# Expert biases of a mixture-of-experts kernel: split in column quarters on 128 partitions and put in place by transfers

## The chip, the cores and the metric

The kernel runs on one core of a Trainium2 chip. The core has five engines with a queue of instructions each: TensorE (PE, matmuls; PEld is its weight load), VectorE (DVE), ScalarE (ACT), GpSimd (POOL) and SyncE (SP), and 16 DMA engines that move what the queues of SP and POOL ask for. Each queue is worked off in the order in which the program was written; engines wait for each other by semaphores. The metric is the time of one execution in microseconds on the device. Line numbers (L130) are those of the kernel before.

## The reference, cut to what matters

One layer for 512 tokens of width 1024: an RMS norm, a projection to four head groups (stick-breaking attention, RG-LRU, HGRN2, Mamba-2), the projection `w_out`, a residual, and then a mixture of 32 experts, four for each token, and a last norm. The biases of the experts come in here:

```python
def run_block(args):
    tok, e = args
    hmid = xt[tok] @ w_gu[e] + b_gu[e]        # b_gu: (32, 2048)
    glu = jnp.minimum(hmid[:, 0::2], SWIGLU_LIMIT)
    lin = jnp.clip(hmid[:, 1::2], -SWIGLU_LIMIT, SWIGLU_LIMIT)
    act = glu * jax.nn.sigmoid(SWIGLU_ALPHA * glu) * (lin + 1.0)
    return act @ w_down[e] + b_down[e]        # b_down: (32, 1024)
```

## The kernel before

The work has a mixer part (about the first 330 us) and an expert part (the rest). The expert part streams the weights of all 32 experts through a ring of buffers (`wch`, 1 MB each) on the SP queue, and multiplies them on PE.

A bias is added by a matmul: a column of ones and zeros that picks the expert, times a table of the biases with the experts on the partitions. For the accuracy of float32 the table of `b_gu` is kept in three bf16 parts that add up to the value: `bgu` is 96 x 2048, part s of expert e on partition 32 s + e. `b_down` is kept in two rounded parts, `bd`, 96 x 1024: the upper part on partitions 0 to 31 and again on 32 to 63, the remainder on 64 to 95. `bgu` is read first by L174, at 318.6 us, `bd` first by L470, at 368.9 us.

`moe_biases` (L119 to L151) makes both tables in the mixer part. Its staging buffer `st` is the ring tile `hg`, 128 x 2048 float32. It loads the 32 rows of a bias three times, one under the other, so that each part is made where it has to lie: for each half of 1024 columns of `b_gu`, ACT rounds 96 rows (L138), DVE subtracts (L139), ACT rounds rows 32 to 63 and 64 to 95 (L141, L142), DVE subtracts on rows 64 to 95 (L143), ACT rounds these (L145). `b_down` is loaded over the first half and made by one ACT and one DVE instruction (L149, L150). The loads go through the POOL queue.

The function is a generator: at each `yield` the program goes on with another. In which order it does is written out by hand, a letter for a step. `m` is `moe_biases`:

```python
ORD1 = 'lcxpvcluelldblllelpmddbcepddssmssmddmbsmddmssm'
ORD2 = 'wnwnwnwwonowwowowwo'
...
emit(ORD1, {"x": xc_silu(), **cgen, "n": nA, "e": c_end(), "l": sL, "d": d_loop(), "s": c_state(), "b": sB,
            "m": moe_biases(tc, a, bp, hg, r_)})
```

Seven `m` stand in `ORD1`. Between them: `d`, the Mamba-2 loop (DVE multiplies the decays by scores, L1874; PE multiplies, L1880; after four rounds DVE makes `y`, L1885 and L1886); `s`, the HGRN2 state (PE L1899, L1906, L1912, L1919; ACT copies `kn`, L1901; DVE updates the state, L1925); `b`, the RG-LRU's norm (ACT L1465, L1466, L1471; DVE L1468, L1472). A letter whose generator is used up does nothing. What is left of the generators after `ORD1` is run out, `b` last but one, ahead of `m`. Then `ORD2` mixes the multiplication by `w_out` (`w`: ACT L1817 and DVE L1818 split 128 x 512 of the weights in two, PE L1823 multiplies) with two norms.

After `ORD2`, SP loads `x` into `acc` (L1958), what the router needs (L98, L100, L102), and then the first expert weights (L159); POOL makes the router's constants (from L69). The router writes the staging buffer `hg` again (L283, first at 290.8 us).

Of the kernel before, what the change touches and what calls it, by code (L numbers as in the profile page):

```python
# [21 lines left out]
F32 = mybir.dt.float32  # L22
FR = mybir.dt.float32r
BF = mybir.dt.bfloat16
I32 = mybir.dt.int32
U32 = mybir.dt.uint32
AF = mybir.ActivationFunctionType
OP = mybir.AluOpType
# [89 lines left out]

def moe_biases(tc, a, bp, st, r_):  # L119

    nc = tc.nc
    bgu = bp.tile([96, 2048], BF, name="bgu")
    bd = bp.tile([96, D], FR, tag="yS", name="bd")
    r_["b"] = bgu, bd
    bst = [st[0:96, 0:1024], st[0:96, 1024:2048]]

    def load(f):
        src = a["moe_b_down"][0] if f == 2 else a["moe_b_gu"][0, :, 1024 * f:1024 * f + 1024]
        for s in range(3):
            nc.gpsimd.dma_start(bst[f % 2][32 * s:32 * s + 32, :], src)  # L130

    load(0)
    load(1)
    yield
    for f in range(2):
        cols = slice(1024 * f, 1024 * f + 1024)
        b = bst[f]
        nc.scalar.activation(bgu[:, cols], b, AF.Copy)  # L138
        nc.vector.tensor_tensor(b, b, bgu[:, cols], op=OP.subtract)  # L139
        yield  # L140
        nc.scalar.activation(bgu[32:64, cols], b[32:64, :], AF.Copy)  # L141
        nc.scalar.activation(bgu[64:96, cols], b[64:96, :], AF.Copy)  # L142
        nc.vector.tensor_tensor(b[64:96, :], b[64:96, :], bgu[64:96, cols], op=OP.subtract)  # L143
        yield
        nc.scalar.activation(bgu[64:96, cols], b[64:96, :], AF.Copy)  # L145
        if f == 0:
            load(2)
    yield
    nc.scalar.activation(bd, bst[0], AF.Copy)  # L149
    nc.vector.tensor_tensor(bd[64:96, :], bst[0][64:96, :], bd[64:96, :].bitcast(F32), op=OP.subtract)  # L150
    yield  # L151


# [898 lines left out]
def tile_kernel(ctx, tc, a, out):  # L1052
# [837 lines left out]
    def c_state():  # L1890
# [3 lines left out]
        for c in range(NT):  # L1894
# [19 lines left out]
            if c < NT - 1:  # L1914
# [13 lines left out]

    emit(ORD1, {"x": xc_silu(), **cgen, "n": nA, "e": c_end(), "l": sL, "d": d_loop(), "s": c_state(), "b": sB,
                "m": moe_biases(tc, a, bp, hg, r_)})  # L1930
    bgu, bd = r_["b"]
    oC = r_["oC"]
# [94 lines left out]
```

## Time and profile before

| | |
|---|---|
| median of 3 runs | 1378.11 us (1372.44 to 1380.81) |
| the profiled execution | 1376.71 us |
| its span, first to last instruction | 1374.9 us |
| mean granted TensorE clock | 0.977 |
| PE / DVE / ACT / POOL busy | 1312.0 / 882.4 / 643.6 / 94.4 us |

Outside the span lie 1.8 us of the profiled execution. Busy times are sums over stages that differ; the views below are cut to the stage that holds the change. In the timeline, several neighbours of one kind can be merged into one row (x4), and rows can overlap by the end of a pipeline. A granted clock of 1.00 is 2.4 GHz, 0.50 is 1.2 GHz.

### The profile page before, as it was taken

The page shows a single profiled execution, that of the slowest core. Times are in us where ns is not written, and L with a number is a line of the kernel's source. Part 1 is how long each engine was busy: PE and PEld are TensorE (multiplying, and loading weights), DVE is VectorE, ACT ScalarE, POOL GpSimd, SP SyncE. Part 2 cuts the span into 40 slices and gives each one's busy share as a digit, 9 for nine tenths or more (in the row PEclk, how much of TensorE's full clock was granted, in tenths as well). Part 3 has the DMA queues.
Part 4 walks back from the last instruction along what each step waited for, and adds up shares of the span by engine and source line. Part 5 has one row for each costly group of instructions (what it writes and reads, how often), then busy time and mean ns, then how long its engine had stood idle before and what let it go on. Part 6 is the DMA issues. An engine that isn't in the chain of part 4 may idle for free.

```text
span 1374.9 us, 17788 instructions
## 1 busy us (share of the span) xinstructions
PE 1312.0 (95%) x6460; PEld 768.3 (56%) x6460; DVE 882.4 (64%) x1215; ACT 643.6 (47%) x886; POOL 94.4 (7%) x162
## 2 busy tenths in 40 slices
PE   7999998898999999999999999999999999999994
PEld 6877773574365554456545655546544555464651
DVE  5457867675576754457546765748545667686865
ACT  5366667652154533336234542526334445454632
POOL 0000123020110002000010000200010000000001
PEclk9999997899999999999999999999999999999998
DMA  6312012087899999888999999999999999999982
GB/s 196 116 61 92 1 70 88 1 325 306 338 398 405 420 419 397 339 363 310 404 366 419 419 394 420 409 419 405 419 400 419 419 393 420 418 417 399 419 359 78
DMA packets 80801, 442.09 MB, mean 322 GB/s; under 512 B 10972, under 2 KB 25380, under 8 KB 31684
## 3 DMA queue, kind: packets, MB, share of 16 engines
q1 hardware_dynamic: 76708, 427.66, 77.7%
q0 software_dynamic: 3856, 12.72, 2.7%
q8 instruction: 52, 0.85, 0.3%
q10 hardware_dynamic: 144, 0.52, 0.1%
q14 instruction: 41, 0.34, 0.1%
HBM read 436.68 MB, written 4.19 MB: 321 GB/s over the span
## 4 chain that ended last, share of the span: by engine, by line
PE 77%; DMA 7%; DVE 7%; ACT 5%; issue 3%; POOL 1%; DVEq 0%; SPq 0%; ACTq 0%; POOLq 0%
PE h L629 18%; PE hL L658 14%; PE m L629 10%; PE m L729 7%; PE m L1198 6%; PE h L789 6%; DMA wch<-in_moe_w_down_dram 4%; DMA wch<-in_moe_w_gu_dram 3%; PE h L658 2%; DVE w L614 1%; PE h L1823 1%; PE m L1823 1%; PE h L696 1%; PE m L1202 1%; PE h L585 1%
## 5 line engine op out<-in xcount | busy, mean ns | idle before, releaser
L614 DVE TENSOR_TENSOR w<-wch,w 128x1024 fp32r<-128x1024 f32 x312 | 378.8, 1224 | 153.8 <-ACT w L613 145.5
L613 ACT ACTIVATE w<-wch 128x1024 fp32r<-128x1024 f32 x312 | 328.4, 1061 | 273.4 <-DMA wch<-in_moe_w_down_dram 98.7
L629 PE MATMUL h<-w,xx 128*72 128x512 f32 (+6 forms) x1248 | 301.9, 399 | 4.9 <-DVE w L614 4.5
L629 PEld LDWEIGHTS h<-w,xx 128*72 128x72 f32 (+6 forms) x1248 | 195.6, 159 | 102.8 <-DVE w L614 7.2
L658 PE MATMUL hL<-wch,xp 128*64 128x512 f32 (+1 forms) x1152 | 239.1, 593 | 1.1 <-DMA wch<-in_moe_w_gu_dram 1.1
L658 PEld LDWEIGHTS hL<-wch,xp 128*64 128x64 f32 (+1 forms) x1152 | 74.8, 134 | 148.8 <-issue 141.2
L729 PE MATMUL m<-wch,aTL 128*64 128x512 f32 x544 | 124.3, 603 | 0.2 <-DVE tg L557 0.2
L629 PE MATMUL m<-w,aH 128*72 128x512 f32 (+6 forms) x416 | 116.5, 400 | 3.4 <-ACT w L613 2.1
L675 ACT ACTIVATE ag<-ag 128x512 f32<-128x512 f32 (+7 forms) x46 | 28.6, 622 | 167.9 <-DVE ag L674 167.8
L629 PEld LDWEIGHTS m<-w,aH 128*72 128x72 f32 (+6 forms) x416 | 62.9, 158 | 39.7 <-issue 7.4
L565 POOL CAST ix<-tg 64x1 int32<-64x1 f32 (+8 forms) x31 | 19.0, 611 | 848.3 <-DVE tg L557 839.7
L791 DVE TENSOR_TENSOR acc<-acc,h 128x1024 f32<-128x1024 f32 (+1 forms) x61 | 72.9, 1198 | 6.4 <-PE h L789 6.4
L729 PEld LDWEIGHTS m<-wch,aTL 128*64 128x64 f32 x544 | 37.0, 138 | 69.2 <-issue 67.2
L763 DVE SCALAR_TENSOR_TENSOR yS<-m,tg,yS 64x512 fp32r<-64x512 f32 (+1 forms) x38 | 28.5, 750 | 71.4 <-ACT yS L761 71.0
L1198 PE MATMUL m<-uH,wh 128*128 128x512 f32 x176 | 71.9, 408 | 0.8 <-DVE uL L1305 0.8
L1198 PE MATMUL m<-uH,wl 128*128 128x512 f32 x176 | 70.1, 398 | 0.5 <-DVE wl L1164 0.4
L1198 PE MATMUL m<-uL,wh 128*128 128x512 f32 x176 | 69.9, 397 | 0.0
L629 PE MATMUL m<-w,aL 128*72 128x512 f32 (+6 forms) x208 | 65.1, 394 | 0.0
L761 ACT ACTIVATE yS<-m,tg 64x512 fp32r<-64x512 f32 (+1 forms) x38 | 25.9, 681 | 74.9 <-PE m L729 72.4
L789 PE MATMUL h<-yS,S 128*128 128x512 f32 (+1 forms) x168 | 54.9, 400 | 2.4 <-DVE acc L791 1.3
L674 DVE TENSOR_SCALAR ag<-hL 128x512 f32<-128x512 f32 (+1 forms) x18 | 11.9, 659 | 64.5 <-PE hL L658 64.5
L1164 DVE TENSOR_TENSOR wl<-wnat,wh 128x1024 fp32r<-128x1024 f32 (+1 forms) x26 | 31.5, 1223 | 30.3 <-ACT wh L1163 30.3
(500 smaller groups left out, 1634.0 us busy)
## 6 DMA issues: line engine op xcount, KB each, us to landing
wch<-in_moe_w_gu_dram SPq DMA_DIRECT2D x256, 1024.0 KB
wch<-in_moe_w_down_dram SPq DMA_DIRECT2D x127, 1024.0 KB
wnat<-in_w_in_dram SPq DMA_DIRECT2D x12, 1024.0 KB
wch<-in_w_out_dram SPq DMA_DIRECT2D x4, 1024.0 KB
xin<-in_x_dram SPq DMA_DIRECT2D x4, 512.0 KB
acc<-in_x_dram SPq DMA_DIRECT2D x4, 512.0 KB
xdr<-wch POOLq DMA_DIRECT2D x4, 512.0 KB, 7.5
out_dram<-fo SPq DMA_DIRECT2D x3, 512.0 KB
```

The costliest lines, as they stand in the source:

```text
L613: nc.scalar.activation(wh, w, AF.Copy)
L614: nc.vector.tensor_tensor(wl, w, wh.bitcast(F32), op=OP.subtract)
L629: nc.tensor.matmul(ps_[q], x, w[:, 512 * q:512 * q + 512], start=start and z == 0, stop=stop and z == 2)
L658: nc.tensor.matmul(u.h[q], u.xT[:, k, :], W[:, 512 * q:512 * q + 512], start=False, stop=last)
L675: nc.scalar.activation(g, g, AF.Gelu_apprx_sigmoid)
L729: nc.tensor.matmul(u.y[0][64 * dh:64 * dh + 64, :], u.aT[:, 2 * (f // 4) + f % 2, (f // 2) % 2, :], W[:, 512 * dh:512 * dh + 512], start=f ...
L763: nc.vector.scalar_tensor_tensor(u.yS[o_, dh, :], y[s_, :], u.gate[s_, :], u.yS[s_, dh, :].bitcast(F32), op0=OP.mult, op1=OP.subtract)
L789: nc.tensor.matmul(hh[:, 512 * dh:512 * dh + 512], s, y, start=z == 0, stop=z == len(todo) - 1)
L791: nc.vector.tensor_tensor(o, o, hh[:, cols], op=OP.add)
L1164: nc.vector.tensor_tensor(wl, w, wh.bitcast(F32), op=OP.subtract)
L1198: nc.tensor.matmul(s.p, s.ws[q // 2][:, k, :], u_[:, k, :], start=(k == 0 and q == 0), stop=(k == KD - 1 and q == 2))
L1823: nc.tensor.matmul(p, m_(x, k)[:, 128 * i:128 * i + 128], ww, start=(k == 0 and q == 0), stop=(k == KD - 1 and q == 2))
```

## The change

The bias rows are loaded once: columns 512 q to 512 q + 511 of `b_gu` go to partitions 32 q to 32 q + 31 of `g`, columns 256 q to 256 q + 255 of `b_down` to the same partitions of `d`. All 128 partitions then hold a quarter each, and the parts of all 2048 columns are made by three ACT and two DVE instructions of 512 columns (`b_down`: one each, 256 columns) in spare columns of the staging buffer. 24 transfers from SBUF to SBUF, 12 on SP's queue for `bgu` and 12 on POOL's for `bd`, put each quarter of each part on its partitions. The generator has four steps in place of seven, so the last three `m` of `ORD1` do nothing.

```diff
-    bst = [st[0:96, 0:1024], st[0:96, 1024:2048]]
-
-    def load(f):
-        src = a["moe_b_down"][0] if f == 2 else a["moe_b_gu"][0, :, 1024 * f:1024 * f + 1024]
-        for s in range(3):
-            nc.gpsimd.dma_start(bst[f % 2][32 * s:32 * s + 32, :], src)
-
-    load(0)
-    load(1)
+    g, d = st[:, 0:512], st[:, 512:768]
+    parts = st[:, 768:1536].bitcast(BF).rearrange("p (s f) -> p s f", s=3)
+    dH, dL = st[:, 1536:1792].bitcast(FR), st[:, 1792:2048].bitcast(FR)
+    for q in range(4):
+        nc.gpsimd.dma_start(g[32 * q:32 * q + 32, :], a["moe_b_gu"][0, :, 512 * q:512 * q + 512])
+        nc.gpsimd.dma_start(d[32 * q:32 * q + 32, :], a["moe_b_down"][0, :, 256 * q:256 * q + 256])
     yield
-    for f in range(2):
-        cols = slice(1024 * f, 1024 * f + 1024)
-        b = bst[f]
-        nc.scalar.activation(bgu[:, cols], b, AF.Copy)
-        nc.vector.tensor_tensor(b, b, bgu[:, cols], op=OP.subtract)
-        yield
-        nc.scalar.activation(bgu[32:64, cols], b[32:64, :], AF.Copy)
-        nc.scalar.activation(bgu[64:96, cols], b[64:96, :], AF.Copy)
-        nc.vector.tensor_tensor(b[64:96, :], b[64:96, :], bgu[64:96, cols], op=OP.subtract)
-        yield
-        nc.scalar.activation(bgu[64:96, cols], b[64:96, :], AF.Copy)
-        if f == 0:
-            load(2)
+    nc.scalar.activation(parts[:, 0, :], g, AF.Copy)
+    nc.scalar.activation(dH, d, AF.Copy)
+    nc.vector.tensor_tensor(g, g, parts[:, 0, :], op=OP.subtract)
+    nc.vector.tensor_tensor(dL, d, dH.bitcast(F32), op=OP.subtract)
     yield
-    nc.scalar.activation(bd, bst[0], AF.Copy)
-    nc.vector.tensor_tensor(bd[64:96, :], bst[0][64:96, :], bd[64:96, :].bitcast(F32), op=OP.subtract)
+    nc.scalar.activation(parts[:, 1, :], g, AF.Copy)
+    nc.vector.tensor_tensor(g, g, parts[:, 1, :], op=OP.subtract)
+    yield
+    nc.scalar.activation(parts[:, 2, :], g, AF.Copy)
+    for s in range(3):
+        for q in range(4):
+            nc.sync.dma_start(bgu[32 * s:32 * s + 32, 512 * q:512 * q + 512], parts[32 * q:32 * q + 32, s, :])
+    for s in range(3):
+        for q in range(4):
+            nc.gpsimd.dma_start(bd[32 * s:32 * s + 32, 256 * q:256 * q + 256], (dH if s < 2 else dL)[32 * q:32 * q + 32, :])
     yield
```

## Rows read from the trace of the kernel before

**Rows 1.** Windows: busy time of PE, PEld, DVE, ACT, POOL, then PEclk, DMA, GB/s

```profile
224.00:251.00 27.00, 19.57 (x153) 9.90 (x151) 15.96 (x27) 16.08 (x28) 4.73 (x10) 0.81 0.16 44
...
700.00:1000.00 300.00, 298.58 (x1419) 164.14 (x1416) 191.46 (x217) 132.09 (x153) 15.11 (x16) 1.00 1.01 411
```

**Rows 2.** Chain of work that ended last, 200 to 330 us: start, us, what

```profile
231.61 1.21 DVE wch L139
232.84 1.06 ACT bgu L141
...
235.01 1.23 DVE wch L143
...
247.92 1.22 DVE bd L150
...
251.95 5.06 PE m L1823 x11
```

**Rows 3.** Timeline, DVE, 222 to 262 us: start, duration, what, idle before

```profile
233.21 0.47 DVE L1925 SCALAR_TENSOR_TENSOR st<-st,gl,p 128x64 f32<-128x64 f32 x2 [0.40 <-PE p L1919]
...
236.25 1.68 DVE L1874 TENSOR_TENSOR wch<-wch,m 128x384 f32<-128x384 f32 x4
...
244.77 0.49 DVE L1874 TENSOR_TENSOR wch<-wch,m 128x128 f32<-128x128 f32 x2
246.03 0.75 DVE L1885 SCALAR_TENSOR_TENSOR y<-xc,dcol,m 128x512 f32<-128x512 f32 x1 [0.78 <-PE m L1880]
...
249.15 0.75 DVE L1468 SCALAR_TENSOR_TENSOR mm<-b,par,rr 128x512 f32<-128x512 f32 x1
250.60 0.69 DVE L1472 TENSOR_TENSOR mL<-mm,mH 128x512 fp32r<-128x512 f32 x1 [0.70 <-ACT mH L1471]
```

**Rows 4.** Timeline, ACT, 222 to 262 us

```profile
230.05 1.04 ACT L138 ACTIVATE bgu<-wch 96x1024 bf16<-96x1024 f32 x1
231.06 0.38 ACT L1901 ACTIVATE kn<-p 128x256 f32<-128x256 f32 x1
...
238.30 0.67 ACT L1465 ACTIVATE rr<-m,eps_t 128x512 f32<-128x512 f32 x1
...
249.94 0.63 ACT L1471 ACTIVATE mH<-mm 128x512 fp32r<-128x512 f32 x1 [3.04 <-DVE mm L1468]
```

**Rows 5.** Timeline, PE, 222 to 262 us

```profile
232.71 0.45 PE L1919 MATMUL p<-vi,kn 128*64 128x64 f32 x8
232.99 1.03 PE L1880 MATMUL m<-wch,xd 128*64 128x512 f32 x4
...
236.87 2.00 PE L1880 MATMUL m<-wch,xd 128*64 128x384 f32 x4 [2.22 <-DVE wch L1874]
...
241.67 0.65 PE L1880 MATMUL m<-wch,xd 128*64 128x256 f32 x4
245.11 0.88 PE L1880 MATMUL m<-wch,xd 128*64 128x128 f32 x4 [2.79 <-DVE wch L1874]
...
251.14 0.79 PE L1823 MATMUL m<-woH,mH 128*128 128x512 f32 x1 [1.45 <-ACT woH L1817]
```

**Rows 6.** Timeline, POOL, 200 to 330 us

```profile
224.04 3.22 POOL L130 DMA_DIRECT2D wch<-in_moe_b_gu_dram  x6
...
276.58 0.56 POOL L69 IOTA it_i<- 128x512 int32 x1 [38.50 <-PE m L1823]
```

**Rows 7.** Instructions of L130: time from issue to landing

```profile
DMA to landing us min/median/max: 2.4/2.9/3.0
```

**Rows 8.** Waits of SP's queue: who waited for whom, us, times, longest

```profile
SPq L1958 <- PE m L1823: 75.6, 1, 75.6
```

**Rows 9.** Windows, columns as in rows 1

```profile
236.00:240.00 4.00, 3.13 (x10) 1.35 (x10) 3.47 (x7) 3.31 (x4) 0.49 (x1) 0.64 0.11 37
...
244.00:257.00 13.00, 9.51 (x41) 6.48 (x42) 8.21 (x14) 6.27 (x10) 0.00 (x0) 0.50 0.00 1
258.00:277.00 19.00, 17.80 (x68) 12.16 (x66) 12.04 (x19) 13.31 (x23) 0.42 (x1) 1.00 0.00 1
```

## Prediction

> **What bounds the kernel now.** I read the windows by stage first, then the chain of work that ended last, then the timeline of each engine in the stretch where the biases are made. In the windows [rows 1] the reader is to see two kinds of stage. From 700 to 1000 us PE is busy 298.58 of 300 us and the DMA engines are full (share 1.01): nothing of the change lies there. From 224 to 251 us, where the seven bias steps run, no engine is full: PE 19.57, DVE 15.96, ACT 16.08 of 27 us, DMA 0.16. Such a stage is bound by engines that hand work to each other, so the chain decides. In it [rows 2] the biases themselves stand on the path: between 231.61 and 249.14 us ten of its pieces are theirs (L139, L143, L141 and L142 twice each, L138 and L150 once), five on DVE at 1.21 to 1.23 us and five on ACT at 1.06 to 1.07, together 5 x 1.22 + 5 x 1.06 = 11.4 us. Nobody needs their result so early; they are on the path because the queues are in order, and the work that is needed stands behind them.
>
> The timelines show that. DVE's L1874 at 236.25, for which PE had been idle for 2.22 us, comes right behind the end of L143 [rows 2, 3, 5]. The next L1874, at 244.77, comes right behind the second L143, and PE's L1880 had waited 2.79 us for it [rows 3, 5]. ACT's L1465 at 238.30 stands behind the second L138, L1468 at 249.15 behind L150 [rows 2 to 4]. At the end of the stretch PE's first L1823 at 251.14 waits for ACT, which waits for that L1468 [rows 4, 5].
>
> **What is removed and added on ACT and DVE.** These engines' times follow the columns, not the partitions: 96 x 1024 takes 1.04 on ACT and 1.21 on DVE, and so does 32 x 1024 (1.06 and 1.23) [rows 2, 4]. ACT had nine instructions, 9 x 1.05 = 9.5 us; it gets three of 512 columns at 0.63 and one of 256 at 0.38 [rows 4], 2.3 us. DVE had five at 1.22, 6.1 us; it gets two of 512 at 0.69 (L1472's time) and one of 256 at 0.42 (a quarter of the row of four L1874) [rows 3], 1.8 us. So 7.2 us go from ACT and 4.3 from DVE; what reaches the end has to be followed along the path.
>
> **The path, step by step.** (1) Loads. POOL issues eight DMAs from 224.04 in place of six; six took 3.22 us, the later ones 0.49 each (3.22 - 0.79 for the first, by 5) [rows 6]. The seventh, the last that the first ACT instruction needs, starts at 227.26 and lands 2.9 us later [rows 7], at 230.2; L138 began at 230.05 [rows 4]. The two ACT instructions then end at about 231.5 instead of 231.1, and `kn` behind them at 231.9 instead of 231.4. PE's L1919, which reads it, is not there before 232.71 [rows 5]: this 0.4 us is hidden.
> (2) DVE subtracts on `g` and `d` until about 232.7 (L139 ended at 232.8), then does L1925 at 233.21 as before, to 233.68 [rows 3]. The second subtraction follows at once, 233.7 to 234.4: its ACT part has been ready since 233.0. The L1874 behind it starts at 234.4, not 236.25: **1.85 us gained**.
> (3) PE then starts the L1880 of 384 columns at about 235.0 instead of 236.87. The old one took 2.00 us, while the one of 512 columns before it took 1.03 [rows 5]: between them the granted clock fell, 0.64 on average from 236 to 240 [rows 9], after the idle 2.22 us, which is now some 0.3. I take the clock as kept here: **1.0 us more**. PE's next L1880, of 256 columns, began 4.80 us after the first [rows 5], now 3.8: at 238.8.
> (4) ACT's L1465 and L1466 were behind L138 until 238.30 and now only behind the third part (0.63): 235.1. DVE's L1468 follows from 239.66 to about 236.4, L1472 ends at 238.6, and the L1874 at 244.77 moves to 238.6. It is no longer the last: the next L1880 of 128 columns waits for PE's own order, 238.8 + 0.65 = 239.5 and not 245.11 [rows 5]. **In all 5.6 us by here.**
> (5) L1885 began 0.92 us after that L1880 [rows 3, 5]: 240.4 instead of 246.03. From there to L1468 it is 3.12 us, 1.22 of which was L150 [rows 2, 3], now gone: L1468 at 242.3 and not 249.15. L1471 and L1823 follow at the old distance of 1.99 us [rows 3 to 5]: first L1823 at 244.3 instead of 251.14, which is 6.85 us, rounded **7.0 us**.
>
> From there everything I know of moves with it: SP's next loads waited 75.6 us for an L1823 and for nothing older [rows 8], POOL's constants likewise, at 276.58 [rows 6]. So the expert weights start earlier by the same amount as PE, and the full DMA engines of the later stage [rows 1] end earlier too.
>
> **The 24 transfers.** No row here is a transfer from SBUF to SBUF. Nearest are the loads of L130: issue 0.49 on POOL, landing 2.4 to 3.0 us [rows 6, 7]; 12 are 5.9 us of issue on each queue, from about 235, done by 244 to 245. What hides it: POOL has nothing until 276.58 and SP nothing until L1958 [rows 6, 8], both 7 us sooner after the change; PE reads `bgu` at 318.6 and `bd` at 368.9, and the staging buffer is overwritten at 290.8. Cost nothing, then; without that cover 5.9 us on SP. The upper end: PE has to take in the ends of 12 transfers at L174 and of 12 at L470, where it took in those of ACT and DVE; no row shows the price of such waits, when all has long landed, and I bound it by one landing, 3.0 us [rows 7]. The lower end is 0, since a wait that is added gains nothing. I take 0: both reads come some 70 and 120 us after the landing.
>
> **The clock at the end of the stretch.** From 244 to 257 us the granted clock was 0.50, 1.2 GHz, although PE was busy 9.51 of the 13 us, and from 258 on 1.00 [rows 9]. It had fallen after the waits of 2.22 and 2.79 us [rows 5]; both all but vanish, but the last links, L1885 to L1823, still leave PE little work for some 4 us. Eleven L1823 took 5.06 us at half the clock [rows 2]; at the full one they would take half, 2.5 us less. I leave this out of the sum, since the light stretch before L1823 stays. The Trainium skill ("TensorE: Matmul & The Clock Gate", Part 1: the HAM clock gate) says that a monitor lets the clock through fully or by half by how busy TensorE has been of late. By that rule, denser work ahead of L1823 may hold 2.4 GHz, and the gain is that of the first rival. The trace agrees that the clock fell after the waits, and cannot say how it goes with shorter ones.
>
> **Sum.** The profiled execution took 1376.71 us (span 1374.9 and 1.8 around it), 1.4 under the median of the three runs: 1376.7 - 7.0 = **1369.7 us**.
>
> **The rivals.**
> *The clock holds too.* TensorE stays at 2.4 GHz from 236 on, and the eleven L1823 are paid at half: 1376.7 - 7.0 - 2.5 = 1367.2. For it: PE has work in most of 224 to 242 us now; against it: the last 4 us.
> *The gain stops halfway.* The path through step 4 has many links (ACT, DVE and PE alternate), and I have set each at its best. If the clock falls as before in step 3 and PE's order or another row of ACT holds `y`, only steps 2 and 5 are gained: 1.85 + 1.22 = 3.1 us, 1373.6. Against it: every instruction on the path that I shortened lies between rows that I can see.
> *The transfers back up, and it is slower.* SP and POOL wait at the first of their 12 until the third part is there, in order; POOL's copies also have to be out of the staging buffer before L283. If each takes the queue not 0.49 but over 4 us, 12 end past 283.8 (290.8 - 7.0), L283 waits, and the router behind it. At 5 us each they end at 295: 11 us late, less the 7 gained, 1380.9. Against it: 2.4 to 3.0 us is the whole way of a load here [rows 7], and they overlap. The same holds for SP, which decides above 2.9 us each (269.7 - 235, by 12).
> *It does not do what it says*, as the pieces saved were not last: 1376.7. The chain names them as last [rows 2].
>
> **How the numbers follow.** Forecast 0.52, clock held 0.23, halfway 0.16, no effect 0.05, slower by the transfers 0.04. The three runs of the kernel before spread over 1372.4 to 1380.8, some 4 us either side, about as much as the cases differ. The range takes the forecast, the held clock (with 1 us on top) and halfway with that spread: 1362 to 1377; the 3.0 us of the transfers' upper end lie inside. A measurement of this kernel tells about 1% (13.8 us) from no change. Faster by that means under 1364.3, which needs the held clock and a run at the low end: 0.08. Slower by that means above 1391.9, the transfers at over 6 us each: 0.02. Within: 0.90.
>
> **What would show it.** In the profile after: L1874 of 384 columns near 234.4, L1880 behind it without 2 us of idle, L1885 near 240.4, first L1823 near 244.3, L1958 near 269.7, all relative to loads that start at 224. The granted clock from 237 to 257 decides between forecast and first rival. I am wrong if the first ACT instruction starts later than about 231 (loads), if L1823 comes early but L1958 does not, or if the expert stage lasts longer by what the mixer saved.

## The result, and the profile after

The change takes 1369.65 us, the median of 15 runs (1364.4 to 1375.94), against 1377.01 us for 15 runs of the kernel before beside it (1371.75 to 1382.28). The ratio is 0.9947, with a 95% interval of 0.9926 to 0.9967: 7.4 us faster, 0.5%, where 7.0 were forecast. The profiled execution took 1368.26 us; its span is 1366.5, 8.4 less than that of before. Outside the bias function, lines of the kernel after have numbers lower by 3 than the same lines before (L1874 is L1871, L1880 is L1877, L1468 is L1465, L1823 is L1820, L1958 is L1955).

Windows of the kernel after, with the columns of [rows 1]; they answer to [rows 1, 9]:

```profile
224.00:251.00 27.00, 24.16 (x177) 14.12 (x176) 15.12 (x32) 13.61 (x31) 10.24 (x21) 0.94 0.20 45
236.00:240.00 4.00, 3.80 (x41) 2.29 (x40) 2.45 (x5) 1.20 (x3) 1.24 (x3) 1.00 0.39 82
240.00:244.00 4.00, 1.72 (x14) 0.81 (x14) 3.27 (x8) 2.06 (x4) 0.00 (x0) 1.00 0.03 8
244.00:257.00 13.00, 12.84 (x43) 9.06 (x44) 6.66 (x11) 7.60 (x14) 0.00 (x0) 0.87 0.00 1
...
700.00:1000.00 300.00, 297.74 (x1415) 163.88 (x1415) 193.96 (x223) 133.47 (x155) 16.79 (x17) 1.00 1.01 413
```

PE fills the bias stretch better, 24.16 of 27 us in place of 19.57, and the granted clock from 236 to 240 is 1.00 in place of 0.64. The thin spot that the prediction named is there: from 240 to 244 PE works 1.72 of 4 us, and behind it the clock falls, though for less long than before: 0.87 on average to 257, in place of 0.50. The stage from 700 to 1000 us is what it was.

The chain of waits of the kernel after, answering to [rows 2]:

```profile
233.79 0.60 DVE wch L139
...
234.91 1.32 PE m L1877 x4
...
239.39 0.76 DVE y L1882
...
243.96 4.40 PE m L1820 x11
```

Of the ten bias pieces in the chain of before, one of 0.60 us is left (L139). Everything else is the mixer's own work.

DVE's timeline after, answering to [rows 3], and then ACT's and PE's, answering to [rows 4] and [rows 5]:

```profile
233.71 0.68 DVE L139 TENSOR_TENSOR wch<-wch 128x512 f32<-128x512 f32 x1
234.31 1.67 DVE L1871 TENSOR_TENSOR wch<-wch,m 128x384 f32<-128x384 f32 x4
236.33 0.75 DVE L1465 SCALAR_TENSOR_TENSOR mm<-b,par,rr 128x512 f32<-128x512 f32 x1 [0.34 <-ACT rr L1463]
...
238.39 0.48 DVE L1871 TENSOR_TENSOR wch<-wch,m 128x128 f32<-128x128 f32 x2
239.39 0.75 DVE L1882 SCALAR_TENSOR_TENSOR y<-xc,dcol,m 128x512 f32<-128x512 f32 x1 [0.53 <-PE m L1877]
...
241.16 0.75 DVE L1465 SCALAR_TENSOR_TENSOR mm<-b,par,rr 128x512 f32<-128x512 f32 x1
```

```profile
229.88 0.38 ACT L1898 ACTIVATE kn<-p 128x256 f32<-128x256 f32 x1 [2.69 <-PE p L1896]
230.16 0.62 ACT L133 ACTIVATE wch<-wch 128x512 bf16<-128x512 f32 x1
...
234.96 0.67 ACT L1462 ACTIVATE rr<-m,eps_t 128x512 f32<-128x512 f32 x1
```

```profile
234.91 1.32 PE L1877 MATMUL m<-wch,xd 128*64 128x384 f32 x4 [0.15 <-DVE wch L1871]
...
238.28 0.97 PE L1877 MATMUL m<-wch,xd 128*64 128x256 f32 x7
...
239.08 0.27 PE L1877 MATMUL m<-wch,xd 128*64 128x128 f32 x1
...
241.11 0.44 PE L1909 MATMUL p<-eG,st 64*64 64x128 f32 x4 [1.31 <-DVE st L1922]
...
243.15 0.50 PE L1820 MATMUL m<-woH,mH 128*128 128x512 f32 x1 [0.86 <-ACT woH L1814]
```

The waits of 2.22 and 2.79 us in front of PE's two L1877 [rows 5] are 0.15 us and none. The first w_out matmul starts at 243.15, 8.0 us before that of the old kernel.

SP's queue and POOL after, where [rows 6, 8] are those of before, and the time from issue to landing of the loads (L130, as [rows 7]), then of POOL's copies (L147):

```profile
230.81 8.58 SPq L144 DMA_DIRECT2D bgu<-wch  x12
267.65 1.77 SPq L1955 DMA_DIRECT2D acc<-in_x_dram  x4
```

```profile
231.38 5.85 POOL L147 DMA_DIRECT2D bd<-wch  x12 [2.99 <-ACT wch L134]
267.60 0.55 POOL L69 IOTA it_i<- 128x512 int32 x1 [30.37 <-PE m L1820]
```

```profile
DMA to landing us min/median/max: 2.1/2.2/2.5
```

```profile
DMA to landing us min/median/max: 1.7/1.8/3.7
```

All 24 transfers are issued by 239.4, and both queues' next work is at 267.6.

Where the gain went from there, each number the start of the first instruction of that line in a profile (for the gate/up matmuls, of the last; the span ends with the last instruction of all):

| us | first w_out matmul | SP's loads (L1955) | first expert matmul | last gate/up matmul | span |
|---|---|---|---|---|---|
| before | 251.14 | 276.65 | 330.0 | 1322.4 | 1374.9 |
| after | 243.15 | 267.65 | 324.3 | 1314.1 | 1366.5 |
| gained | 8.0 | 9.0 | 5.7 | 8.3 | 8.4 |

Some 3.3 us of the gain are lost between SP's loads and the experts, and come back by the end of the expert stage. In the kernel after, PE's timeline and the windows (columns as [rows 1]) of the router's stretch show where they are lost:

```profile
311.03 2.51 PE L285 MATMUL h<-rw,hT 128*128 128x32 f32 x16 [0.86 <-DVE hT L277]
313.35 3.76 PE L325 MATMUL m<-wch,G 128*128 128x512 f32 x4
...
317.92 3.75 PE L325 MATMUL m<-wch,G 128*128 128x512 f32 x4 [0.71 <-DVE G L308]
```

```profile
312.00:314.00 2.00, 2.00 (x10) 1.82 (x10) 1.20 (x8) 0.95 (x1) 0.00 (x0) 0.57 0.96 399
314.00:318.00 4.00, 3.29 (x9) 1.14 (x7) 1.98 (x10) 0.19 (x1) 0.53 (x1) 0.50 0.33 131
...
324.00:326.00 2.00, 2.00 (x8) 0.55 (x8) 0.69 (x1) 0.11 (x1) 0.00 (x0) 0.52 0.93 389
```

The same lines and windows of the kernel before, which had no row ahead of the prediction:

```profile
320.09 1.97 PE L288 MATMUL h<-rw,hT 128*128 128x32 f32 x16 [0.86 <-DVE hT L280]
321.90 3.26 PE L328 MATMUL m<-wch,G 128*128 128x512 f32 x4
...
325.97 1.95 PE L328 MATMUL m<-wch,G 128*128 128x512 f32 x4 [0.71 <-DVE G L311]
```

```profile
321.00:323.00 2.00, 2.00 (x12) 1.49 (x12) 1.57 (x10) 0.89 (x1) 0.00 (x0) 0.86 0.97 403
...
326.00:328.00 2.00, 1.92 (x4) 0.62 (x4) 0.04 (x1) 0.04 (x1) 0.01 (x1) 1.00 0.00 0
```

The router's matmuls begin 9.06 us earlier (311.03 for 320.09) behind the same wait of 0.86 us. Then the clock stays at 1.2 GHz until about 326 in the one, over 13 us, and for some 3 us in the other: two L325 groups of 3.76 and 3.75 us stand where 3.26 and 1.95 stood.

### The profile page after: what moved, and what is told of

The parts are those of the page before. It is cut to its first block, busy times and chain, and to the rows that moved or that the text cites. A ratio compares the mean times of both kernels' runs of the same rounds, so it can differ in the third digit from the quotient of the medians.

```text
span 1366.5 us, 17829 instructions
## 1 busy us (share of the span) xinstructions
PE 1309.0 (96%) x6460; PEld 766.6 (56%) x6460; DVE 877.5 (64%) x1213; ACT 636.5 (47%) x881; POOL 100.5 (7%) x173
## 4 chain that ended last, share of the span: by engine, by line
PE 79%; DMA 7%; DVE 7%; ACT 4%; issue 2%; POOL 1%; SPq 0%; DVEq 0%; ACTq 0%; POOLq 0%
PE h L626 18%; PE hL L655 15%; PE m L626 11%; PE m L726 8%; PE m L1195 6%; PE h L786 6%; DMA wch<-in_moe_w_down_dram 3%; DMA wch<-in_moe_w_gu_dram 3%; PE h L655 2%; DVE w L611 1%; PE h L1820 1%; PE h L693 1%; PE m L1820 1%; PE m L1199 1%; PE m L325 1%
## 5 line engine op out<-in xcount | busy, mean ns | idle before, releaser
L786 PE MATMUL h<-yS,S 128*128 128x512 f32 (+1 forms) x168 | 55.9, 413 | 1.9 <-DVE acc L788 0.8
```

Of the source, the lines that this page charges most:

```text
L786: nc.tensor.matmul(hh[:, 512 * dh:512 * dh + 512], s, y, start=z == 0, stop=z == len(todo) - 1)
```

## The experiments

The theory under test: the time gained is that of the bias instructions on DVE's and ACT's queues ahead of the mixer's last links, and the transfers cost nothing. The rivals: the transfers cost or save something of their own; or the gain is mainly TensorE's clock.

One measure is the same for all. DVE's COPY into `st` (L1920 of the kernel after) starts at 231.33 before and 231.44 after, ahead of all that changed on DVE's queue; from it I count to the first w_out matmul and to SP's loads, so that what differs ahead of it, some 2 us between the profiles, drops out. The ratio is that of the times, of 6 to 15 runs of each kernel, to the kernel before beside it.

| kernel | copy of `st` to first w_out matmul, us | copy of `st` to SP's loads, us | ratio to before, 95% interval |
|---|---|---|---|
| before | 19.81 | 45.32 | |
| after | 11.71 | 36.21 | 0.9947 [0.9926, 0.9967] |
| after_again | 11.69 | 36.18 | 0.9945 [0.9926, 0.9964] |
| bd_alone | 18.79 | 43.25 | 1.0004 [0.9983, 1.0025] |
| bgu_alone | 13.11 | 38.48 | 0.9962 [0.9944, 0.9981] |
| no_bias | 10.92 | 36.33 | 0.9918 [0.989, 0.9946] |
| no_copies | 11.70 | 36.18 | 0.9948 [0.9928, 0.9969] |
| copies_x3 | 11.70 | 34.61 | 0.9934 [0.991, 0.9957] |
| dose | 16.36 | 41.90 | 0.9976 [0.9958, 0.9995] |
| tail_later | 11.70 | 36.18 | 0.9918 [0.99, 0.9937] |
| fill_mixer | 11.80 | 34.60 | 0.9917 [0.9896, 0.9939] |
| fill_router | 11.70 | 36.18 | 0.9949 [0.9933, 0.9966] |
| all_fills | 11.80 | 34.62 | 0.9908 [0.9887, 0.9928] |
| tail_before | 19.80 | 45.39 | 0.9987 [0.9969, 1.0004] |

**after_again**: the kernel after, unchanged, beside other kernels.

> The changed kernel once more, as the measure for the kernels beside it on the same chip. In the first profile the first L1820 (w_out) started at 243.15 us, the next loads of SP at 267.65, the first matmul of the experts at 324.3, the span ended at 1366.5. Path theory (the gain is made by 243 us, and the end moves with it): again 243 and 267.5 to 268, and 1369 to 1371 us. Clock theory for what lies behind (the clock falls to 1.2 GHz in some light stretches behind 300 us, for longer or shorter from run to run): the mixer part repeats within 1 us, the start of the experts and the end do not, by 3 us and more.

Measured: 1367.25 us for 12 runs, 0.9945, a little under the 1369 to 1371 that were expected. The two distances repeat to 0.03 us. Its profiled execution, however, took 1373.68 us: its experts begin at 321.3, 3.0 us ahead of those in the first profile, its last gate/up matmul starts at 1314.3, 0.2 us later than there, and then its last stretch is 5.2 us longer. PE's timeline and a window of the end (columns as [rows 1]), first of this run, then of the first profile of the kernel after:

```profile
1334.77 0.47 PE L786 MATMUL h<-yH,S 72*128 72x512 f32 x1 [1.45 <-DVE S L767]
...
1336.00:1349.00 13.00, 13.00 (x30) 4.91 (x30) 4.85 (x4) 0.00 (x0) 0.00 (x0) 0.52 0.00 0
```

```profile
1335.25 0.47 PE L786 MATMUL h<-yH,S 72*128 72x512 f32 x1 [1.46 <-DVE S L767]
...
1333.00:1349.00 16.00, 13.19 (x52) 4.82 (x48) 8.31 (x10) 2.82 (x4) 0.00 (x0) 1.00 0.09 28
```

PE's wait ahead of both is the same, 1.45 and 1.46 us at L786 for DVE's L767; behind it the clock falls in the one and not in the other. So 5 us of one execution say nothing about the change, and medians are needed.

**bd_alone**: the kernel before, with only `b_down` in quarters and copied.

```diff
+    d, dH, dL = st[:, 0:256], st[:, 256:512].bitcast(FR), st[:, 512:768].bitcast(FR)
...
-    nc.scalar.activation(bd, bst[0], AF.Copy)
-    nc.vector.tensor_tensor(bd[64:96, :], bst[0][64:96, :], bd[64:96, :].bitcast(F32), op=OP.subtract)
+    nc.scalar.activation(dH, d, AF.Copy)
+    nc.vector.tensor_tensor(dL, d, dH.bitcast(F32), op=OP.subtract)
+    for s in range(3):
+        for q in range(4):
+            nc.gpsimd.dma_start(bd[32 * s:32 * s + 32, 256 * q:256 * q + 256], ...)
```

> Only the biases of the down projection are split in quarters and put in place by 12 transfers of POOL; the others are made as before. Path theory: of the ten pieces only the last (1.22 us on DVE, now 0.42) gets shorter, so the first w_out matmul starts at 250.3 instead of 251.1 and the time is 0.8 us below that of before, not to be told from it: 1376. Rival (what counts is the work taken from ACT and DVE, wherever it stands): ACT and DVE lose 1.45 of the 11.5 us that the whole change takes from them, so an eighth of the gain, about 1 us: no difference to the path theory here, but there is one in the run with the other half.

Measured: first w_out matmul at 250.49, a gain of 1.02 us on the common measure. In time that can't be told from before, as expected: a ratio of 1.0004, with 1 inside its interval (medians 1373.92 and 1375.28 us). DVE's timeline shows the one instruction of step 5, 0.41 us where L150 took 1.22 [rows 2]:

```profile
248.18 0.41 DVE L155 TENSOR_TENSOR wch<-wch 128x256 fp32r<-128x256 f32 x1
```

**bgu_alone**: the kernel after, with `b_down` made on 96 rows again, in the seventh step, in two halves of 512 columns.

```diff
+    for x in range(2):
+        nc.scalar.activation(bd[:, 512 * x:512 * x + 512], d[x], AF.Copy)
+    for x in range(2):
+        o = bd[64:96, 512 * x:512 * x + 512]
+        nc.vector.tensor_tensor(o, d[x][64:96, :], o.bitcast(F32), op=OP.subtract)
```

> Only the biases of the first projection are split in quarters and put in place by 12 transfers of SP; those of the down projection are loaded three times and made on 96 rows in two halves of 512 columns, in the last of the seven steps. Path theory: two DVE instructions of 0.69 stand again ahead of the norm of the second half, so the first w_out matmul starts 1.4 us later than in the changed kernel, at 244.6, and the time is 1.4 us above the changed kernel's: about 1371. Rival (transfers on POOL's queue or the down biases' earlier place matter): more than 3 us apart.

Measured: first w_out matmul at 244.41; 1.40 us of the gain of 8.10 are lost, and 6.70 are those of `b_gu`. The cause stands in DVE's timeline, in front of L1470 as the path has it:

```profile
241.13 1.28 DVE L152 TENSOR_TENSOR bd<-wch,bd 32x512 fp32r<-32x512 f32 x2
242.43 0.75 DVE L1470 SCALAR_TENSOR_TENSOR mm<-b,par,rr 128x512 f32<-128x512 f32 x1
```

The two parts alone, 1.02 and 6.70, make 7.7 of the 8.10 us.

**no_bias**: neither loads nor parts; both tables are set to zero.

```diff
+    nc.gpsimd.memset(bgu, 0.0)
+    nc.gpsimd.memset(bd.bitcast(F32), 0.0)
     yield
```

> The biases are left out: both tables are set to zero by POOL, with no loads, no ACT and DVE steps and no transfers, so the output lacks them. Path theory: in the changed kernel only DVE's second subtraction (0.60 us) and little else of the biases is left on the path, so this is at most 1 us faster than the changed kernel: first w_out matmul at 242.3 to 243.1, time 1368 to 1370. Rival (the change left part of the cost in place, in transfers, waits of PE on them or in SP's queue): 3 us or more below the changed kernel, and the stretch after 243 us is shorter.

Measured: 0.79 us less than the kernel after to the first w_out matmul, and nothing to SP's loads (36.33 for 36.21; the clock fell earlier here, to 0.50 from 242 to 244 us). What is left of the biases costs the path up to w_out 0.8 us. The time, 1362.85 us for 6 runs, misses the 1368 to 1370 that were expected and is more below the kernel after than that: 0.9918 for 0.9945. The intervals overlap, and no_copies, next, isn't faster; what the other 3 us are stays open.

**no_copies**: the parts are made, but the 24 transfers are left out, and the tables are zero.

```diff
-            nc.sync.dma_start(bgu[32 * s:32 * s + 32, 512 * q:512 * q + 512], parts[32 * q:32 * q + 32, s, :])
...
-            nc.gpsimd.dma_start(bd[32 * s:32 * s + 32, 256 * q:256 * q + 256], ...)
```

> The changed kernel without its 24 transfers: loads, ACT and DVE steps stay, both tables are set to zero by POOL, so the output lacks the biases. Path theory with hidden transfers: the same milestones and time as the changed kernel (first w_out matmul 243.2, SP's loads 267.5, 1367 to 1370 us); the 3 to 4 us by which the kernel without any bias work was faster are then 1.3 us of path and the spread of six runs. Rival (transfers are not free: SP's queue, or PE's waits on their ends): as fast as the kernel without bias work, 1363 to 1364, with the first w_out matmul still at 243.2.

Measured: 1369.32 us for 9 runs, and both distances of the kernel after. Without the transfers nothing is gained.

**copies_x3**: every transfer three times.

```diff
-    for s in range(3):
+    for s in 3 * (0, 1, 2):
```

> The changed kernel with each of its 24 transfers issued three times, 36 on SP and 36 on POOL. In the changed kernel SP's 12 take 230.8 to 239.4 us and POOL's 231.4 to 237.2; three times that ends near 257 and 249, still ahead of SP's loads at 267.5. Path theory with hidden transfers: no change, 1367 to 1370 us, the first w_out matmul at 243.2. Rival: each 12 more cost as much as the first 12, so 3 us or more above the changed kernel for the 48 that are added.

Measured: 1366.31 us for 7 runs. The ratio is 0.9948 without the transfers, 0.9934 with 72 of them and 0.9945 to 0.9947 with 24. SP's and POOL's rows of copies_x3 show the cover:

```profile
230.67 23.87 SPq L144 DMA_DIRECT2D bgu<-wch  x36
265.92 1.77 SPq L1955 DMA_DIRECT2D acc<-in_x_dram  x4
```

```profile
231.25 17.57 POOL L147 DMA_DIRECT2D bd<-wch  x36 [4.25 <-ACT wch L134]
265.83 0.56 POOL L69 IOTA it_i<- 128x512 int32 x1 [17.02 <-DVE mL L1469]
```

36 issues end on SP at 254.5, on POOL at 248.8, and there are still 11 and 17 us to the next work. That SP's loads come 1.60 us sooner than after has another cause. PE's timeline of copies_x3, and a window of it (columns as [rows 1]):

```profile
240.97 0.44 PE L1909 MATMUL p<-eG,st 64*64 64x128 f32 x4 [1.30 <-DVE st L1922]
...
243.01 0.51 PE L1820 MATMUL m<-woH,mH 128*128 128x512 f32 x1 [0.86 <-ACT woH L1814]
```

```profile
243.00:250.00 7.00, 6.69 (x26) 4.93 (x27) 4.42 (x8) 4.54 (x8) 5.82 (x12) 1.00 0.59 118
```

PE's waits are those of the kernel after, 1.30 and 0.86 us, but the clock stays at 1.00 behind them, and the eleven w_out matmuls take 2.80 us in the chain in place of 4.40. This is the prediction's first rival, in one profile, with nothing on PE's path changed. In the five profiles with the same path and no more than 24 transfers (after, after_again, no_copies, tail_later, fill_router) the clock fell each time; whether chance or the 48 added transfers kept it here is not shown.

**dose**: the kernel after, with dead work on ACT and DVE in four of the seven steps.

```diff
+    def more(n):
+        for _ in range(n):
+            nc.scalar.activation(g, g, AF.Copy)
+        for _ in range(2):
+            nc.vector.tensor_tensor(g, g, g, op=OP.subtract)
...
     nc.scalar.activation(parts[:, 2, :], g, AF.Copy)
+    more(1)
...
+    more(2)
+    yield
+    nc.scalar.activation(g, g, AF.Copy)
+    yield
+    more(1)
```

> The changed kernel with idle work put back where the old steps stood: ACT copies and DVE subtractions of 512 columns on the staging buffer that nobody reads, in the fourth step one and two, in the fifth two and two, in the sixth one and none, in the seventh one and two (ACT 3.2 us, DVE 4.1 us in all; the removed work was 7.2 and 4.3). Path theory: they stand ahead of needed work in the queues again, the first w_out matmul moves to 246.5 to 249, SP's loads by as much, and the time is 3 to 6 us above the changed kernel: 1371 to 1375. Rival (the gain came from the loads or from something else than the queue's order): less than 1.5 us at the first w_out matmul.

Measured: 16.36 us to the first w_out matmul, 4.65 more than after, inside what the path gave. DVE's and then PE's timeline of dose:

```profile
238.42 1.42 DVE L134 TENSOR_TENSOR wch<-wch 128x512 f32<-128x512 f32 x2 [0.76 <-ACT wch L132]
239.76 0.48 DVE L1885 TENSOR_TENSOR wch<-wch,m 128x128 f32<-128x128 f32 x2
```

```profile
240.09 0.89 PE L1891 MATMUL m<-wch,xd 128*64 128x128 f32 x4 [2.87 <-DVE wch L1885]
```

The wait of 2.79 us of the kernel before [rows 5] is back, 2.87 us, and the clock is at 1.2 GHz behind it again: four matmuls of 128 columns take 0.89 us, as before (0.88). SP's loads are 5.69 us later than after, and the time is 1374.57 us, as expected, or 0.9976, some 4 us over after's 0.9945 by the ratios, though the intervals just overlap. The path moves also when work is put in, and the time goes the same way.

**tail_later** and **tail_before**: in the last loop, the adding of the expert before the last is put one turn later; in the kernel after and in the kernel before.

```diff
-        if f < NT:
-            add(pending, f)
+        if 0 < f <= NT:
+            add(pending, f - 1)
```

> The changed kernel with one edit at its end: each addition to the output (L786) stands one matmul step later, so that PE has work in the 1.45 us in which it waited for DVE near 1334 us. In the runs with a long end the granted clock fell to 1.2 GHz right after that wait, for 13 us (58 us from the last first-projection matmul to the end, 52 otherwise). Clock theory: the long end goes, the runs' spread shrinks at the top (few above 1371), the median is 2 to 5 us below the changed kernel: 1362 to 1366. Rival (the clock falls there whatever PE does): same spread and at most 1 us from the shorter wait.

> The kernel before with the later additions at the end and nothing else. It takes the long end of some runs out of the comparison: the change is then worth this run minus the changed kernel with the same edit (0.9918 of before). Path theory: 7 to 8 us between the two, so this one at 0.997 to 0.998 of before, about 1372.5. Rival (part of the measured gain was a luckier end): less than 5 us between them.

Measured: 1365.65 us for 6 runs (1362.61 to 1366.82), 0.9918; in the kernel before 0.9987. PE's wait ahead of the last stretch, in tail_later:

```profile
1333.07 0.47 PE L786 MATMUL h<-yH,S 72*128 72x512 f32 x1 [0.60 <-DVE S L767]
```

The wait is 0.60 us and not 1.46, and from the last gate/up matmul to the end it is 50.7 us in place of 52.4. That the clock doesn't fall any more can't be said from six runs: fill_mixer and fill_router, which leave the end alone, had no run over 1369.01 us in six either. With the edit in both kernels the change is worth 0.9918 / 0.9987 = 0.9931, which agrees with 0.9947 within the intervals: 9.5 us, where 7 to 8 were expected.

**fill_mixer**: in the thin spot, 6 small matmuls and 4 of 512 columns on banks that are overwritten afterwards, to keep PE at work (the kernel that ran has these ten, and not the one more that the expectation names).

```diff
+                for _ in range(3 if c == NT - 1 and ti == 0 else 0):
+                    for hh in range(2):
+                        nc.tensor.matmul(oC[0][64 * hh:64 * hh + 64, t0:t0 + 128], ..., start=True, stop=True)
...
+    for _ in range(4):
+        nc.tensor.matmul(pa[0][0], m_(0, 0)[:, 0:128], m_(0, 1), start=True, stop=True)
     th0 = wo_steps(pa, 0)
```

> The changed kernel with matmuls added in the waits of PE ahead of w_out whose results are overwritten: six of 128 columns ahead of the wait for DVE's state, four of 512 ahead of the wait for the first w_out part, one more in the next wait. In the changed kernel the clock stood at 1.2 GHz for the first eight or so w_out matmuls (eleven took 4.40 us). Clock theory: the clock stays at 2.4 GHz, the eleven take 2.6 to 3 us, SP's loads start 1.5 us earlier and the time is 1 to 2 us below the changed kernel's 0.9946 of before. Rival (the clock falls there anyway, or what follows waits for ACT): the eleven again 4 us and more, same time.

Measured: 1364.52 us for 6 runs, 0.9917. Its windows, columns as [rows 1]:

```profile
240.00:244.00 4.00, 3.70 (x22) 2.42 (x23) 3.22 (x6) 3.17 (x7) 0.00 (x0) 1.00 0.00 0
244.00:257.00 13.00, 11.99 (x45) 7.95 (x44) 7.66 (x12) 8.65 (x15) 0.00 (x0) 1.00 0.00 1
```

PE is busy 3.70 of the 4 us and the clock holds: the eleven w_out matmuls take 2.80 us, and SP's loads come 1.61 us sooner than after, as in copies_x3, though the w_out matmuls don't start earlier (11.80). all_fills, with the same ten matmuls, repeats it (34.62). Since copies_x3 held the clock without them, two profiles make it likely, not certain, that the ten did it. The time gained, some 4 us by the ratios, is more than that; the intervals of the two ratios overlap, so only the 1.6 us are seen.

**fill_router**: the same idea ahead of the router's bias matmuls.

```diff
+    for _ in range(4):
+        nc.tensor.matmul(h[0], sel.to_broadcast([96, 64]), c["bgu"][:, 0:512], start=True, stop=True)
```

> The changed kernel with four matmuls of 512 columns added, whose result is overwritten, ahead of the first expert's bias in the router, where PE then waits 0.86 us; the clock fell to 1.2 GHz about 1.5 us after that wait, for 3 to 13 us. Clock theory: the clock falls there less often, the experts start within 52 to 54 us of SP's loads (324.3 - 267.5 = 57 in the first profile of the changed kernel, 54 in the second and before); the time moves by less than that, since the weight stream sets the end of the expert stage: 0 to 2 us. Rival (small matmuls and transposes around it lower the clock, not the wait): no change of the distance.

Measured: 0.9949, no change against after. Its first expert matmul starts 48.9 us behind the first weight load, in the two profiles of the kernel after 53.3 and 50.2; but fill_mixer and copies_x3 have the same 48.9 without this edit, so that nothing is shown of it.

**all_fills**: both fills and the later tail.

> The changed kernel with both kinds of added matmuls and the later additions at the end. If the three are worth what the theory says one by one: 4 of the end, 1.5 of the mixer, 0 to 2 of the router, so 1360 to 1364 us, 0.988 to 0.991 of before, and few runs above 1366. Rival (only the end counts, what is gained ahead of the expert stage is lost in it): 0.9918 as with the end alone.

Measured: 1360.91 us (1357.64 to 1364.09), 0.9908 [0.9887, 0.9928]: 12.7 us under the kernel before by the ratio, and the lowest median of all kernels here. It is inside what was expected, but the rival (the end alone, 0.9918) lies in its interval too, so that this run doesn't decide between them. Its mean clock in the profiled run is 0.986, where after has 0.980 and before 0.977.

## Why the prediction was right, point by point

**What bounds the stretch.** Shown. Bias instructions taken out of the queues (`b_down` alone, `b_gu` alone), nearly all taken out, and put back as dead work move the first w_out matmul as the path says: 1.02, 6.70 and 8.10 us earlier than before (8.89 with no bias work left), and of the 8.10 us 4.65 back. In time, by the ratios, `b_down` alone gains nothing that can be told, `b_gu` alone 5.2 us, the kernel after 7.3, and with the dead work 3.3 are left. The rival that the gain is mainly TensorE's clock is right for a smaller part: of the 8.10 us, some 2 are matmuls at 2.4 in place of 1.2 GHz (an estimate from steps 3 and 5 below: 4.80 to 3.37 us, and some 0.5), and so is most of the 1.0 us from there to SP's loads. The rest are bias instructions gone from the queues.

**Step 1, the loads.** ACT's first instruction was forecast at 230.2 and began at 230.16, but for another reason: a load landed 2.1 to 2.5 us after its issue, not 2.9, so that the last one needed was there by 229.9, and what stood ahead was `kn` in ACT's own queue, at 229.88. The number was luck.

**Steps 2 and 4.** Right within 0.2 us: the second subtraction 233.71 (233.7), L1871 of 384 columns 234.31 (234.4), L1462 234.96 (235.1), L1465 236.33 (236.4), L1871 of 128 columns 238.39 (238.6).

**Steps 3 and 5: the mechanism right, the size short by 1.15 us.** The clock kept, which step 3 took as likely, is what 236 to 240 show. But two terms still held the old clock. The 256-column L1877 comes 3.37 us behind the 384-column one, and not 3.8, since the matmuls between the two also ran at 2.4 GHz: L1850 took 0.49 us where it had taken 0.80. (The 384-column ones themselves took 1.32 us and not 1.03; DVE's L1871, which feeds them, took 1.67.) And the 0.92 us from the last L1880 to L1885 in step 5 was a distance at 1.2 GHz: the four matmuls of 128 columns took 0.88 [rows 5], and here single ones take 0.27 and overlap. L1882 began at 239.39 and not 240.4. The two later distances were right, 1.77 us to L1465 (1.90) and 1.99 to w_out (1.99). So the first w_out matmul started at 243.15, not 244.3.

**The clock at the end of the stretch: part of the first rival.** It fell behind the thin spot, as the forecast had it, but came back after some 3.4 us (0.87 over 13 us: 13 x 0.13 / 0.5) and not after 13. The eleven matmuls took 4.40 in place of 5.06 us. Hence SP's loads at 267.65 and not 269.7. The rival in full is seen in copies_x3 and in fill_mixer: another 1.6 us to SP's loads, and the eleven in 2.80 us, 2.3 less than before where the prediction had 2.5. The Trainium skill ("TensorE: Matmul & The Clock Gate", Part 1: The HAM clock gate) has the clock pass fully or by half according to how busy TensorE has been of late. fill_mixer agrees with it, 1.00 throughout with PE at 3.70 of 4 us; copies_x3 held 1.00 with waits like those of after, where it fell, so that the wait's length alone doesn't decide here.

**"From there everything I know of moves with it": the step that failed in part.** SP's loads and POOL's constants moved by 9.0 us, but the first expert matmul by 5.7 in one profile and 8.7 in the other. The prediction had no term for the clock in the router's stretch, which fell behind an unchanged wait of 0.86 us for some 3 us before and over 13 us in the first profile after. All 14 profiles show what it costs there: with a mean granted clock of 1.00 over the 58 to 59 us behind the first weight load (L156), the first expert matmul comes 48.9 to 49.0 us behind that load (four profiles), with 0.97 50.0 to 50.4 (five), with 0.94 51.5 (one) and with 0.88 53.2 to 53.3 (four). In the two profiles of the kernel after it cost nothing in the end: the last gate/up matmul starts at 1314.1 and 1314.3, 8.3 and 8.1 us earlier than before, although PE's start differs by 3.0. What exactly sets the end of that stage isn't settled: over the 14 profiles it comes 1038.4 to 1045.7 us behind the first weight load and 989.4 to 994.2 behind the first expert matmul, neither of which is fixed enough to tell.

**The transfers.** Cost 0, as taken: with none and with 24 of them SP's loads come at the same distance to 0.03 us, and with none, 24 and 72 the times agree within intervals of some 3 us either way. The issue on SP was dearer than the 0.49 us that I used, 8.58 / 12 = 0.72 us, and still 28 us from the next work. The landings of POOL's copies, 1.7 to 3.7 us, reach beyond the 3.0 us used as the bound of one. The Trainium skill ("DMA: Bandwidth & Descriptors", Anatomy of one DMA — SWDGE (gpsimd) path) gives about 2.0 us and the bytes by 436 GB/s for a DMA that POOL issues; that makes an estimate of 2.15 us for the 64 KB of a load of `b_gu`, and the trace has 2.1 to 2.5 with a median of 2.2.

**The other rivals.** The gain didn't stop halfway. That the transfers back up was far off: SP would have had to take over 2.9 us for each.

**The total.** 1369.65 us beside 1369.7 is in part luck: the path gave 1.1 us more than forecast up to w_out and 2.1 up to SP's loads, and of these 9.1 us the medians keep 7.4, for which no run names the cause. The interval of the ratio reaches from 4.5 to 10.2 us, and single executions of the same kernel differ by up to 11.5.

## What to carry to other kernels

An instruction whose result nobody needs yet can still set the time when the work that is needed stands behind it in an in-order queue; read it from the chain, and cut such work by its columns, since the time here followed the columns and not the partitions. Transfers on queues that are idle can then put the parts in place for nothing, as long as the next work on those queues is further off than their issues. And when a gain of some us is followed along the path, ask of each distance at which clock it was measured: terms taken over from the profile before carried 1.2 GHz into a stretch that now ran at 2.4.

## What was not expected of the hardware

- A short wait of PE was followed by 1.2 GHz in one execution of a program and not in the next, with the same wait: 1.45 and 1.46 us at the end of the kernel (over 13 us at half clock, or none). In the mixer, waits of 1.30 and 0.86 us were followed by it in five profiles and not in that of copies_x3, which is another program.
- The time of a run goes with its mean granted clock. Of the 15 runs of the kernel after, the eight with 0.979 to 0.984 took 1364.4 to 1369.69 us, the seven with 0.973 to 0.977 took 1369.65 to 1375.94.
- Transfers from SBUF to SBUF took SP 0.72 us of issue each on average, where its four loads took 1.77 / 4 = 0.44, and POOL 5.85 / 12 = 0.49, the same as for loads.
